# Two heads' scores in turn on half the rows of TensorE, without stacked operands, and all PSUM accumulators from one group of eight banks

## The chip, the core and the metric

One core of a Trainium2 chip runs the whole program, which is one launch. The metric is the device time of that launch in microseconds (us); lower is better. The engines are named as in the profile: PE is TensorE's matmul, PEld its weight load, DVE is VectorE, ACT is ScalarE, POOL is GpSimd, SP is SyncE, which here only issues DMAs. PE writes into PSUM, which has eight banks of 128 x 512 f32.

## The reference

Two layers over 512 tokens of width 1024. Each layer is a half-step SwiGLU, a mixer, and a second half-step SwiGLU, each between two RMS norms. The change lies in the mixer:

```python
proj = u @ w_in[l]
qa, ka, va, qb, kb, vb, qc, kc, vc, gl = jnp.split(proj, split_at, axis=-1)
oa = neighbourhood_attention(qa, ka, va, na_rpb[l])      # 8 heads of 64, windowed, a bias per head
ob = sliding_window_attention(rope(qb), rope(kb), vb, sw_sink[l])   # 8 query heads, 2 kv heads, |i-j| <= 128
oc = differential_attention(rope(qc), rope(kc), vc, lam, ...)       # 4 heads of two maps: p0 - lam * p1, dense
gates = jax.nn.sigmoid(gl + b_gate)
merged = sum(gates[n] * (branch[n] @ w_branch[l, n]) for n in range(3))
h = h + rmsnorm(merged @ w_out[l], mix_post_g[l])
```

All of it is float32. The head width is 64.

## The kernel before

**Precision.** Every operand of a matmul is split into a high and a low part (`split`: ACT writes hi, DVE writes lo = x - hi), and a product is made of hi*hi, hi*lo and lo*hi (`mm3`, lines 298 to 300, PSUM tiles `mm`). A projection of one block of 128 columns is `dense1`: 8 blocks of depth, so 24 matmuls of 128x512. The weights stream in and are split in halves of a tile by ACT (line 199) and DVE (line 200).

**Units of the mixer.** The table `ORDER` lists the units of a mixer, and `do` writes them in that order. `qa`, `qb`, `qc` project q, k, v; `aa`, `ab`, `ac` are the attention units: `aa0` to `aa3` and `ab0` to `ab3` hold a pair of heads each, `ac0` to `ac3` one differential head with two maps. `ga`, `gb`, `gc` are gate projections, `ya`, `yb`, `yc` the branch products, `fc` closes a differential head. A part of the table is `qb0 ga4 ga5 ga7 ya5 ga3 ga6 ab0 qb1 ya1`. In the mixer a scheduler puts the instructions of each engine into a fixed order when the program is built; what is written earlier goes first, as far as its inputs and its buffers are there. Each engine then runs its list in order. In the feed-forward phases and at the mixer's end the order is set by hand.

**PSUM.** `bank(tag)` takes a bank from one of three groups: `mm` (4 banks, projections), `at` (3 banks, scores and transposes) and `o` (1 bank, attention output).

**Scores before.** A head has 64 rows, so `stacks` makes operands of 128 rows by DMA on SP: `st` holds hi over lo, and for k also `sw` with lo over hi. Two matmuls (lines 1337 and 1338, in C 1475 and 1476) then give all four products. `softmax_pv` runs for one head at a time: for each of four blocks of 128 queries the scores, then DVE adds the bias and takes the minimum (line 1341), ACT takes the exponential (1350), DVE scales rows (1357), PE transposes (1365), ACT and DVE split the transposed blocks (324, 325), PE multiplies with v (1368, 1369), and ACT and DVE join the two halves of the output (1371, 1372). B has a sink logit in between (1347, 1353, 1354). `attn_c` takes maxima (1477), scales them (1478), exponentials (1482), joins two maps (1487, 1490), transposes (1498) and multiplies (1501 to 1503). `turn` transposes v on PE (1318) from a copy that `plain` makes on ACT (1425).

Of the kernel before, what the change touches and what calls it, by code (L numbers as in the profile page):

```python
# [2 lines left out]

# [1 line left out]

# [5 lines left out]
F32 = mybir.dt.float32  # L11
F32R = mybir.dt.float32r
# [97 lines left out]
def encoder_kernel(ctx: ExitStack, tc: tile.TileContext, order, xT, wts, cols, rows, rpb, consts, tables, out):  # L110
# [7 lines left out]
    phase = [None]  # L118

    BUFS = {"X": 6, "n": 2, "wr": 3, "wp": 4}  # L120
    ABUFS = {"f": {"t": 4, "x": 10}, "m": {"t": 5, "h": 4, "rr": 2, "tx": 5, "st": 16, "g": 10, "s": 2, "pt": 4}}
    PBUFS = {"mm": 4, "at": 3, "o": 1}

    def open_phase(kind):
        pool = ExitStack()
# [5 lines left out]
    def nm(s):  # L131
        serial[0] += 1
        return f"{s}{serial[0]}"

    def big(tag, dt=F32, shape=(P, T), name="v"):
        if tag in BUFS:
            return sb.tile(list(shape), dt, tag=tag, name=nm(name), bufs=BUFS[tag])
        kind, pool = phase[0]
        return pool.tile(list(shape), dt, tag=tag, name=nm(name), bufs=ABUFS[kind][tag])

# [1 line left out]
        return sb.tile([P, w], F32, tag=tag, name=nm(tag), bufs=bufs)  # L142

    def bank(tag):
        return ps.tile([P, T], F32, tag=tag, name=nm(tag), bufs=PBUFS[tag])

    V, A, G, PE = nc.vector, nc.scalar, nc.gpsimd, nc.tensor

    def f(t):
        return t.bitcast(F32)  # L150
# [1145 lines left out]
        return ap.rearrange("p (j r c) -> p j r c", r=8, j=4)  # L1296


    def stacks(x, both):
        hi, lo = split(x, "tx")  # L1300
        res = []
        for s in range(2):
            own = slice(64 * s, 64 * s + 64)
            st = big("st", F32R, name="st")
            nc.sync.dma_start(f(st)[0:64], f(hi)[own])
            nc.sync.dma_start(f(st)[64:128], f(lo)[own])
            sw = None
            if both:
                sw = big("st", F32R, name="sw")
                nc.sync.dma_start(f(sw)[0:64], f(lo)[own])  # L1310
                nc.sync.dma_start(f(sw)[64:128], f(hi)[own])
            res.append((st, sw))
        return res

    def turn(x, heads):
        tp = bank("at")
# [9 lines left out]
            return lambda j, s: v[j // 2][:, j % 2, s, :]  # L1326
        return split(tp, "st")

    def softmax_pv(sq, sk, vof, bias, scale, sink, odst, oview):
        ss, nmx = [], small("nmx")  # L1330
        sall, at = big("s", shape=(P, NT * T), name="s"), 0
        for i in range(NT):
            j0, j1 = window(i)
            n = (j1 - j0) * P
            sp = bank("at")[:, :n]
            qs = sq[0][:, i * P : (i + 1) * P]
            PE.matmul(sp, qs, sk[0][:, j0 * P : j1 * P], start=True, stop=False)
            PE.matmul(sp, qs, sk[1][:, j0 * P : j1 * P], start=False, stop=True)
            s = sall[:, at : at + n]
            at += n  # L1340
            V.tensor_tensor_reduce(
                out=s, in0=sp, in1=bias(i), scale=-1.0, scalar=3e38, op0=ALU.add, op1=ALU.min,
                accum_out=nmx[:, i : i + 1],
            )
            ss.append(s)
        if sink is not None:
            V.tensor_scalar(out=nmx, in0=nmx, scalar1=scale, scalar2=sink[1], op0=ALU.mult, op1=ALU.min)
        l = small("l")
        for i in range(NT):
            A.activation(ss[i], ss[i], AF.Exp, scale=-scale, bias=nmx[:, i : i + 1], accum_out=l[:, i : i + 1])  # L1350
        if sink is not None:
            es = small("es", 4, 3)
            A.activation(es, nmx, AF.Exp, bias=sink[0])
            V.tensor_tensor(out=l, in0=l, in1=es, op=ALU.add)
        V.reciprocal(out=l, in_=l)
        for i in range(NT):
            V.tensor_scalar(out=ss[i], in0=ss[i], scalar1=l[:, i : i + 1], scalar2=None, op0=ALU.mult)
        op = bank("o")
        for j in range(NT):
            i0, i1 = window(j)  # L1360
            n = (i1 - i0) * P
            tp = bank("at")[:, :n]
            for i in range(i0, i1):
                c = (j - window(i)[0]) * P
                PE.transpose(tp[:, (i - i0) * P : (i - i0 + 1) * P], ss[i][:, c : c + P], ident)  # L1365
# [5 lines left out]
        A.activation(t, op[64:128, :], AF.Copy)  # L1371
        V.tensor_tensor(out=odst, in0=oview(op[0:64, :]), in1=oview(t), op=ALU.add)
# [14 lines left out]
    def mixer(l, op, first):  # L1387
# [40 lines left out]
        OT = {}  # L1428

        def qkv_a(q, k, v):  # L1430
            sq, sk = stacks(plain(q, True, 0.125), False), stacks(plain(k, True), True)
            return sq, sk, turn(plain(v, True), 2)

        oa = [sb.tile([P, 4, T], F32R, tag="X", name=nm("oa"), bufs=BUFS["X"]) for _ in range(2)]

        def attn_a(p, sq, sk, vof):
            o = big("t", name="o")
            for s in range(2):
                softmax_pv(
                    sq[s], sk[s], lambda j, s=s: vof(j, s), biases(2 * p + s), 1.0, None,  # L1440
                    perm(o[64 * s : 64 * s + 64, :]), natural,
                )
# [7 lines left out]
        def attn_b(p, sq, skb, vofb):  # L1450
            o = big("t", name="o")
            for s in range(2):
                hd = 2 * p + s
                kv = hd // 4
                softmax_pv(
                    sq[s], skb[kv], lambda j, kv=kv: vofb(j, kv), bias_b, 0.125,
                    (sink[:, l, hd : hd + 1], nsink[:, l, hd : hd + 1]),
                    o[64 * s : 64 * s + 64, :], lambda ap: ap,
                )
            OT["b", p] = split(o, "g")  # L1460

        oc, totc = [], []

        def attn_c(sq, sk, v):
            vh, vl = v
            aa = []
            sall = big("s", shape=(P, NT * T), name="s")
            for i in range(NT):
                pm = []
                lc = small("lc", 2)  # L1470
                nm2 = small("nm2", 2)
                for s in range(2):
                    sp = bank("at")
                    qs = sq[s][0][:, i * P : (i + 1) * P]
                    PE.matmul(sp, qs, sk[s][0], start=True, stop=False)
                    PE.matmul(sp, qs, sk[s][1], start=False, stop=True)
                    V.tensor_reduce(out=nm2[:, s : s + 1], in_=sp, axis=AX.X, op=ALU.max)
                    V.tensor_scalar(
                        out=nm2[:, s : s + 1], in0=nm2[:, s : s + 1], scalar1=-0.125, scalar2=None, op0=ALU.mult
                    )  # L1480
                    e = big("tx", name="e") if s else sall[:, i * T : (i + 1) * T]
                    A.activation(
                        e, sp, AF.Exp, scale=0.125, bias=nm2[:, s : s + 1], accum_out=lc[:, s : s + 1]
                    )
                    pm.append(e)
                V.reciprocal(out=lc, in_=lc)
                V.tensor_scalar(
                    out=pm[1], in0=pm[1], scalar1=lc[:, 1:2], scalar2=nlam[:, l : l + 1], op0=ALU.mult, op1=ALU.mult
                )
                V.scalar_tensor_tensor(  # L1490
                    out=pm[0], in0=pm[0], scalar=lc[:, 0:1], in1=pm[1], op0=ALU.mult, op1=ALU.add
                )
                aa.append(pm[0])
# [40 lines left out]
                    G.tensor_tensor(out=merged[m], in0=merged[m], in1=t, op=ALU.add)  # L1534

        def qkv_b(c):
            return stacks(rope(dense1(w, l, c, X), cosR, sinR), c == KB)

        def qkv_c(hd):
            sq = stacks(rope(dense1(w, l, QC + hd, X), cosR, sinR), False)  # L1540
            sk = stacks(rope(dense1(w, l, KC + hd, X), cosR, sinR), True)
            return sq, sk, turn(plain(dense1(w, l, VC + hd, X), False), 1)

        def finish_c(hd):
            A.activation(totc[hd], totc[hd], AF.Sqrt)
# [37 lines left out]
        for u in ORDER.split():  # L1583
# [1 line left out]
        M = [split(merged[m], "st", 0.5) for m in range(KD)]  # L1585


        hN = [big("s", shape=(P, 2, 2, T), name="h") for _ in range(2)]
# [4 lines left out]
        H = Handover(  # L1593
            l, "mix_post_g", (1.0, 1.0), ("ffn2_pre_g", l), gains, lambda tb, n: hN[tb // 2][:, tb % 2, n, :],
            lambda tb, n: ys[tb][n], True, [accs[0:2], accs[2:4]] * 2,
        )
        at = len(order) // HB
# [126 lines left out]
```

## Time and profile before

| | |
|---|---|
| median of 3 runs | 2442.7 us (2439.57 to 2444.72) |
| profiled execution, its own time | 2441.57 us |
| its span (first to last instruction) | 2439.8 us |
| PE busy | 2404.1 us (99%) |
| DVE busy | 1797.8 us (74%) |
| ACT busy | 1347.5 us (55%) |
| DMA queue issues of `st` and `sw` from SP | 84 + 84 + 36 + 36 |

PE's busy time is a union of records whose ends are modelled, so the distance from the start of one matmul to the start of the next is what a matmul costs in a stream. For DVE and ACT a record ends after the next has begun, by some 0.08 us on DVE.

### The profile page before, as it was taken

Reading aid. Unit: us, or ns where it says so; the run is one execution under the profiler, and the core shown is the slowest. Engines: PE = TensorE matmul, PEld = TensorE weight load, DVE = VectorE, ACT = ScalarE, POOL = GpSimd, SP = SyncE. Lnnn points to the kernel's source line nnn. Section 1 sums busy time; section 2 is a strip of 40 time slices with the busy share of each in tenths; the row PEclk is TensorE's granted clock in tenths of the full one; section 3 lists DMA queues with packets and bytes.
Section 4 is the critical chain, followed back from the end, with each engine's and each line's share of the span. In section 5 each row is a group of like instructions: output and inputs, shape, how many; then the busy total and the mean of one; then the engine's idle time right before and its main releaser. Section 6 shows DMA issues by size and latency. Waiting matters only on the chain. (4 is left out here: it accounts for less than half of the span.)

```text
span 2439.8 us, 37786 instructions
## 1 busy us (share of the span) xinstructions
PE 2404.1 (99%) x14298; PEld 2111.5 (87%) x14298; DVE 1797.8 (74%) x2943; ACT 1347.5 (55%) x2471; POOL 192.1 (8%) x192
## 2 busy tenths in 40 slices
PE   9999999999999999999999999999999999999998
PEld 8999888888877889998899998888877778899987
DVE  8887976857667467888878878776676764788786
ACT  6555655646555365555655555555465554555553
POOL 0111000000111100110001110000001111011100
PEclk9999999999999999999999999999999999999999
DMA  5566536445442334654435565373454333356642
GB/s 170 162 163 182 169 132 175 116 113 149 111 131 95 111 105 132 169 154 162 170 95 157 156 173 190 116 183 106 113 143 124 110 103 121 96 147 165 184 144 87
DMA packets 119190, 340.59 MB, mean 140 GB/s; under 512 B 15968, under 2 KB 22752, under 8 KB 118496
## 3 DMA queue, kind: packets, MB, share of 16 engines
q1 hardware_dynamic: 91344, 224.85, 29.9%
q10 hardware_dynamic: 22032, 79.78, 10.9%
q0 software_dynamic: 5632, 33.56, 6.8%
q8 instruction: 112, 1.84, 0.3%
q14 instruction: 70, 0.57, 0.1%
HBM read 285.16 MB, written 48.23 MB: 137 GB/s over the span
## 5 line engine op out<-in xcount | busy, mean ns | idle before, releaser
L298 PE MATMUL mm<-X,w 128*128 128x512 f32 (+1 forms) x1044 | 397.1, 380 | 2.2 <-ACT w L199 1.7
L299 PE MATMUL mm<-X,w 128*128 128x512 f32 (+1 forms) x1044 | 396.8, 380 | 0.7 <-DVE X L522 0.7
L300 PE MATMUL mm<-X,w 128*128 128x512 f32 (+1 forms) x1044 | 396.1, 380 | 0.0
L200 DVE TENSOR_TENSOR w<-wr,w 128x512 fp32r<-128x512 f32 x360 | 255.3, 714 | 168.2 <-ACT w L199 167.0
L199 ACT ACTIVATE w<-wr 128x512 fp32r<-128x512 f32 x360 | 223.4, 627 | 226.6 <-PE mm L300 184.3
L842 PE MATMUL mm<-ht,l 128*128 128x256 f32 x1120 | 316.5, 283 | 0.0
L842 PE MATMUL mm<-ht,h 128*128 128x256 f32 x1120 | 316.3, 282 | 0.0
L842 PE MATMUL mm<-lt,h 128*128 128x256 f32 x1120 | 315.6, 282 | 0.0
L298 PEld LDWEIGHTS mm<-X,w 128*128 128x128 f32 x1044 | 197.4, 189 | 34.0 <-ACT w L199 1.9
L299 PEld LDWEIGHTS mm<-X,w 128*128 128x128 f32 x1044 | 197.2, 189 | 32.2 <-DVE X L522 1.1
L300 PEld LDWEIGHTS mm<-X,w 128*128 128x128 f32 x1044 | 197.1, 189 | 31.4
L842 PEld LDWEIGHTS mm<-ht,l 128*128 128x128 f32 x1120 | 213.1, 190 | 0.0
L842 PEld LDWEIGHTS mm<-ht,h 128*128 128x128 f32 x1120 | 213.0, 190 | 0.0
L842 PEld LDWEIGHTS mm<-lt,h 128*128 128x128 f32 x1120 | 212.7, 190 | 0.0
L1082 PE MATMUL mm<-wh,f 128*128 128x512 f32 x640 | 200.3, 391 | 0.0
L842 PE MATMUL mm<-X,h 128*128 128x256 f32 x1120 | 200.3, 279 | 0.0
L842 PEld LDWEIGHTS mm<-X,h 128*128 128x128 f32 x1120 | 171.2, 189 | 0.3
L842 PE MATMUL mm<-X,l 128*128 128x256 f32 x560 | 155.4, 278 | 0.0
L1082 PEld LDWEIGHTS mm<-wh,f 128*128 128x128 f32 x640 | 120.3, 188 | 26.9
L702 DVE TENSOR_TENSOR l<-wr,h 128x1024 fp32r<-128x1024 f32 x70 | 85.7, 1224 | 78.5 <-PE mm L842 78.5
L1082 PE MATMUL mm<-wl,f 128*128 128x512 f32 x320 | 126.6, 396 | 3.1 <-DVE wl L959 3.1
L324 ACT ACTIVATE hi<-at 128x256 fp32r<-128x256 f32 (+2 forms) x168 | 77.2, 474 | 73.4 <-PE at L1365 37.9
(366 smaller groups left out, 5458.5 us busy)
## 6 DMA issues: line engine op xcount, KB each, us to landing
wr<-in_wts_dram SPq DMA_DIRECT2D x223, 512.0 KB, 4.7
wr<-in_wts_dram ACTq DMA_DIRECT2D x152, 512.0 KB, 3.6
sum<-in_wts_dram POOLq DMA_DIRECT2D x64, 512.0 KB, 5.5
st<-hi SPq DMA_DIRECT2D x84, 128.0 KB, 2.5
st<-lo SPq DMA_DIRECT2D x84, 128.0 KB, 3.4
ap<-in_wts_dram SPq DMA_DIRECT2D x20, 512.0 KB, 6.7
a<-kept SPq DMA_DIRECT2D x32, 256.0 KB, 5.9
ap<-sum SPq DMA_DIRECT2D x16, 512.0 KB, 4.7
```

What stands on the lines that cost most here:

```text
L199: A.activation(hi, raw, AF.Copy)
L200: V.tensor_tensor(out=lo, in0=raw, in1=f(hi), op=ALU.subtract)
L298: PE.matmul(acc, w[0], x[0], start=start, stop=False)
L299: PE.matmul(acc, w[0], x[1], start=False, stop=False)
L300: PE.matmul(acc, w[1], x[0], start=False, stop=stop)
L324: A.activation(hi, src, AF.Copy)
L702: V.tensor_tensor(out=W[g]["l1"], in0=raws[g][0], in1=f(W[g]["h1"]), op=ALU.subtract)
L842: PE.matmul(acc, ws[i], xs[j], start=start and k == n == 0, stop=stop and k == HK - 1 and n == 2, skip_group_check=True,)
L1082: PE.matmul(acc, x[i], w[j], start=start and n == 0, stop=stop and n == 2, skip_group_check=True)
```

## The change

`stacks` goes. `parts` splits q and k into hi and lo and leaves them where they are, two heads on 64 rows each; only B's shared k is doubled by DMA (`kv`, two heads' worth of the same 64 rows). `scores` writes six matmuls for a pair of heads, three products each, alternating between rows 0 to 63 and rows 64 to 127, each queued behind the one before with `issue_after`. `attend` writes the scores and minima of both heads for all four query blocks first, and then `softmax_pv` for one head and for the other. `bank` takes every accumulator from one group of eight. Tile `s` is narrower and comes three times, `tx` six times. `ORDER` stays.

```diff
-    PBUFS = {"mm": 4, "at": 3, "o": 1}
+BANKS = 8
+SW = 10 * P
...
     def bank(tag):
-        return ps.tile([P, T], F32, tag=tag, name=nm(tag), bufs=PBUFS[tag])
+        return ps.tile([P, T], F32, tag="bank", name=nm(tag), bufs=BANKS)
...
-    def stacks(x, both):
-        hi, lo = split(x, "tx")
...
+    def parts(x, twice=False):
+        if not twice:
+            return split(x, "st")
...
+    def scores(q, k, i, ks):
+        out = [bank("at")[:, : ks.stop - ks.start] for _ in range(2)]
+        queue = []
+        qs = slice(i * P, (i + 1) * P)
+        for n, (x, y) in enumerate(((0, 0), (0, 1), (1, 0))):
+            for s in range(2):
+                own = slice(64 * s, 64 * s + 64)
+                with tc.issue_after(queue[-1]) if queue else nullcontext():
+                    mm = PE.matmul(out[s], q[x][own, qs], k[y][own, ks], start=n == 0, stop=n == 2)
+                queue.append(mm.ins)
+        return out
...
+    def attend(q, k, vof, bias, scale, sinks, odst, oview):
+        ss, nmx = [[], []], [small("nmx") for _ in range(2)]
+        sall, at = [big("s", shape=(P, SW), name="s") for _ in range(2)], 0
+        for i in range(NT):
+            j0, j1 = window(i)
+            n = (j1 - j0) * P
+            for s, sp in enumerate(scores(q, k, i, slice(j0 * P, j1 * P))):
+                ss[s].append(sall[s][:, at : at + n])
+                V.tensor_tensor_reduce(
+                    out=ss[s][i], in0=sp, in1=bias[s](i), scale=-1.0, scalar=3e38, op0=ALU.add, op1=ALU.min,
+                    accum_out=nmx[s][:, i : i + 1],
+                )
+            at += n
+        for s in range(2):
+            softmax_pv(ss[s], nmx[s], lambda j, s=s: vof(j, s), scale, sinks and sinks[s], odst[s], oview)
```

In the changed file the line numbers are a little higher: the scores are line 1322, the transposes 1377, the products with v 1380 and 1381; in C the transposes are 1502, the products 1505 to 1507.

**PE at `ab0` of layer 0.** `at` are score and transpose banks, `mm` a projection's bank, `s` the softmax rows, `o` the output's bank. Before, the last scores of the first head and what follows, up to the first transposes:

```order
L1338 MATMUL at_5521<-sw_5110,st_5315 128x384
L1337 MATMUL at_5525<-st_5107,st_5315 128x256
L1338 MATMUL at_5525<-sw_5110,st_5315 128x256
L298 MATMUL mm_5663<-X_3642,w_5477 128x512
L299 MATMUL mm_5663<-X_3643,w_5477 128x512
L300 MATMUL mm_5663<-X_3642,w_5477 128x512
...
L299 MATMUL mm_5663<-X_3645,w_5494 128x512
L1365 MATMUL at_5544<-cons,s_5512 128x128
L1365 MATMUL at_5553<-cons,s_5512 128x128
```

Now:

```order
L1322 MATMUL at_5500<-kv_5067,hi_5271 128x256
L1322 MATMUL at_5499<-kv_5068,hi_5271 128x256
L1322 MATMUL at_5500<-kv_5068,hi_5271 128x256
L1322 MATMUL at_5499<-kv_5067,lo_5272 128x256
L1322 MATMUL at_5500<-kv_5067,lo_5272 128x256
L1377 MATMUL at_5524<-cons,s_5467 128x128 x2
L1380 MATMUL o_5523<-hi_5527,v_5119 128x256
L1377 MATMUL at_5533<-cons,s_5467 128x128 x2
L1381 MATMUL o_5523<-lo_5528,v_5119 128x256
```

Before, 23 matmuls of a projection stand between the first head's last score and its first transpose; now the 24 scores of both heads stand in one piece and the first transpose comes right behind them. The next projection's first matmul stands 21 rows further on, among the second head's products with v.

**PE at `ac0` of layer 0.** `s` holds the joined maps of two query blocks, `hi`, `lo` of `o` are split transposes. Before, among the last scores:

```order
L1475 MATMUL at_6887<-st_6669,st_6615 128x512
L1476 MATMUL at_6887<-sw_6672,st_6615 128x512
L300 MATMUL mm_6983<-hi_5938,w_6813 128x512
L1475 MATMUL at_6893<-st_6675,st_6618 128x512
L1476 MATMUL at_6893<-sw_6678,st_6618 128x512
L298 MATMUL mm_6983<-hi_6405,w_6813 128x512
...
L1498 MATMUL at_6904<-cons,s_6830 128x128
L298 MATMUL mm_7001<-X_3642,w_6966 128x512
```

Now:

```order
L1322 MATMUL at_6826<-hi_6609,lo_6562 128x512
L1322 MATMUL at_6827<-hi_6609,lo_6562 128x512
L1502 MATMUL at_6845<-cons,s_6762 128x128 x2
L1502 MATMUL at_6845<-cons,s_6763 128x128 x2
L1505 MATMUL o_6844<-hi_6850,hi_6653 128x512
L1502 MATMUL at_6857<-cons,s_6762 128x128 x2
L1502 MATMUL at_6857<-cons,s_6763 128x128 x2
```

Before, branch products and projections stand between scores and transposes and among the transposes; now nothing does, from the first score of the unit to its sum of squares (line 1515), which is the last of the unit on PE. The other eleven attention units of a mixer read the same way (where two attention units follow each other in `ORDER`, the scores of the second are mixed into the last products of the first), and so does `turn`: its transposes stand right behind the last matmul of the projection that they turn.

**DVE at `ab0`.** `nmx` are the row minima, `l` the row sums, `es` the sink's term. Before, the first head's last minima and what follows:

```order
L1341 ISA s_5512,nmx_5511<-at_5525,cons 128x256
L1341 ISA nmx_5511 128x1
L200 TENSOR_TENSOR w_5681<-wr_5679,w_5681 128x512
L1347 TENSOR_SCALAR nmx_5511<-nmx_5511,nsink 128x4
L1354 TENSOR_TENSOR l_5530<-l_5530,es_5535 128x4
L1355 RECIPROCAL l_5530<-l_5530 128x4
```

Now, with `s_5467` for the first and `s_5468` for the second head:

```order
L1349 ISA s_5467,nmx_5465<-at_5499,cons 128x256
L1349 ISA nmx_5465 128x1
L1349 ISA s_5468,nmx_5466<-at_5500,cons 128x256
L1349 ISA nmx_5466 128x1
L1359 TENSOR_SCALAR nmx_5465<-nmx_5465,nsink 128x4
L1359 TENSOR_SCALAR nmx_5466<-nmx_5466,nsink 128x4
L1366 TENSOR_TENSOR l_5510<-l_5510,es_5515 128x4
L1367 RECIPROCAL l_5510<-l_5510 128x4
```

The second head's minima have moved ahead of the first head's sums and scaling. One split of a weight (line 201) stands among the eight minima of this unit.

The order of PE in the feed-forward phases is the same as before. SP issues 16 DMAs for `kv` in place of 240 for `st` and `sw`.

More of the change, by code (lines that the diff above doesn't have):

```diff
@@ L1 @@
 import math
-from contextlib import ExitStack
+from contextlib import ExitStack, nullcontext
 import numpy as np
@@ L1296, in natural @@
         return ap.rearrange("p (j r c) -> p j r c", r=8, j=4)
-    def stacks(x, both):
-        hi, lo = split(x, "tx")
+    def parts(x, twice=False):
+        if not twice:
+            return split(x, "st")
+        own = split(x, "tx")
         res = []
         for s in range(2):
[L1303 to L1312, printed above, removed]
-        return res
+            pair_ = [big("st", F32R, name="kv") for _ in own]
+            for dst, src in zip(pair_, own):
+                for at in range(2):
+                    nc.sync.dma_start(f(dst)[64 * at : 64 * at + 64], f(src)[64 * s : 64 * s + 64])
+            res.append(tuple(pair_))
+        return res
+    def scores(q, k, i, ks):
[9 more added lines that the diff above has]
+        return out
     def turn(x, heads):
@@ L1334, in softmax_pv @@
             n = (j1 - j0) * P
[L1335 to L1339, printed above, removed]
-            at += n
[L1341 to L1345, printed above, removed]
+            for s, sp in enumerate(scores(q, k, i, slice(j0 * P, j1 * P))):
[4 more added lines that the diff above has]
+                )
+            at += n
+        for s in range(2):
+            softmax_pv(ss[s], nmx[s], lambda j, s=s: vof(j, s), scale, sinks and sinks[s], odst[s], oview)
+    def softmax_pv(ss, nmx, vof, scale, sink, odst, oview):
         if sink is not None:
@@ L1430, in qkv_a, with attn_a @@
         def qkv_a(q, k, v):
-            sq, sk = stacks(plain(q, True, 0.125), False), stacks(plain(k, True), True)
-            return sq, sk, turn(plain(v, True), 2)
+            return parts(plain(q, True, 0.125)), parts(plain(k, True)), turn(plain(v, True), 2)
         oa = [sb.tile([P, 4, T], F32R, tag="X", name=nm("oa"), bufs=BUFS["X"]) for _ in range(2)]
-        def attn_a(p, sq, sk, vof):
+        def attn_a(p, q, k, vof):
             o = big("t", name="o")
[L1438 to L1442, printed above, removed]
+            attend(
+                q, k, vof, [biases(2 * p + s) for s in range(2)], 1.0, None,
+                [perm(o[64 * s : 64 * s + 64, :]) for s in range(2)], natural,
+            )
             OT["a", p] = tuple(t[:, p, :] for t in oa)
@@ L1448, in bias_b, with attn_b, attn_c @@
             return maskB[:, P:] if i == 0 else maskB[:, : 2 * P] if i == NT - 1 else maskB
-        def attn_b(p, sq, skb, vofb):
+        def attn_b(p, q, kb, vofb):
             o = big("t", name="o")
[L1452 to L1459, printed above, removed]
+            kv = p // 2
+            attend(
+                q, kb[kv], lambda j, s: vofb(j, kv), [bias_b] * 2, 0.125,
+                [(sink[:, l, hd : hd + 1], nsink[:, l, hd : hd + 1]) for hd in (2 * p, 2 * p + 1)],
+                [o[64 * s : 64 * s + 64, :] for s in range(2)], lambda ap: ap,
+            )
             OT["b", p] = split(o, "g")
         oc, totc = [], []
-        def attn_c(sq, sk, v):
+        def attn_c(q, k, v):
             vh, vl = v
             aa = []
-            sall = big("s", shape=(P, NT * T), name="s")
+            sall = [big("s", shape=(P, SW), name="s") for _ in range(2)]
             for i in range(NT):
@@ L1471, in attn_c @@
                 nm2 = small("nm2", 2)
[L1472 to L1476, printed above, removed]
+                for s, sp in enumerate(scores(q, k, i, WHOLE)):
                     V.tensor_reduce(out=nm2[:, s : s + 1], in_=sp, axis=AX.X, op=ALU.max)
@@ L1480, in attn_c @@
                     )
[L1481 removed]
+                    e = big("tx", name="e") if s else sall[i // 2][:, i % 2 * T : i % 2 * T + T]
                     A.activation(
@@ L1585, in mixer @@
         M = [split(merged[m], "st", 0.5) for m in range(KD)]
-        hN = [big("s", shape=(P, 2, 2, T), name="h") for _ in range(2)]
+        hN = []
+        for _ in range(NT - 1):
+            h = big("s", shape=(P, SW), name="h")
+            hN.append([h[:, :T], h[:, T : 2 * T]])
+        hN.append([big("tx", name="h") for _ in range(2)])
         ys = [[big(tag, name="y") for tag in ("h", "t")] for _ in range(NT)]
```

14 lines of the change are left out of this document (5 added, 9 removed).

## The prediction

> **What bounds the kernel now.** I read the page first, then the busy time of the two mixers, PE's waits, and then one attention unit instruction by instruction.
>
> ```profile
> span 2439.8 us, 37786 instructions
> PE 2404.1 (99%) x14298; PEld 2111.5 (87%) x14298; DVE 1797.8 (74%) x2943; ACT 1347.5 (55%) x2471; POOL 192.1 (8%) x192
> 360.00:800.00 440.00, 431.79 (x2154) 354.65 (x2154) 297.62 (x686) 243.19 (x531) 33.50 (x23) 1.00 0.46 127
> 1573.00:2015.00 442.00, 433.90 (x2142) 354.95 (x2141) 297.15 (x684) 244.19 (x532) 35.55 (x24) 1.00 0.46 128
> PE at L1337 <- DVE nmx L1341: 2.7, 2, 1.5
> ```
>
> The third and fourth rows are the two mixers: length, then busy time of PE, PEld, DVE, ACT. PE is idle for 440.00 - 431.79 = 8.2 us in one and 8.1 us in the other, 16.3 us in all. So PE sets the time, in the mixers too, and a wait of a score for the softmax before it costs 2.7 us in the whole run. The next rows say what a matmul costs in a stream: the chain of waits merges equal pieces, and 24 of 512 columns take 5.51 us (0.230 each), 72 of 256 take 8.47 us (0.118), 8 transposes 0.90 us (0.11).
>
> ```profile
> 1556.09 5.51 PE mm L1082 x24
> 2146.39 8.47 PE mm L842 x72
> 1688.33 0.90 PE at L1365 x8
> ```
>
> Why PE does not wait is seen at `ab0`, first PE, then DVE and ACT (start, duration, both in us):
>
> ```profile
> 519.99 0.28 PE L1338 MATMUL at<-sw,st 128*128 128x256 f32 x1
> 520.11 0.34 PE L1337 MATMUL at<-st,st 128*128 128x384 f32 x1
> 520.46 0.34 PE L1337 MATMUL at<-st,st 128*128 128x384 f32 x1
> ...
> 521.02 0.28 PE L1338 MATMUL at<-sw,st 128*128 128x256 f32 x1
> 521.14 0.39 PE L298 MATMUL mm<-X,w 128*128 128x512 f32 x1
> ...
> 526.16 0.39 PE L299 MATMUL mm<-X,w 128*128 128x512 f32 x1
> 526.39 0.87 PE L1365 MATMUL at<-cons,s 128*128 128x128 f32 x6
> ```
>
> ```profile
> 520.31 0.42 DVE L1341 CUSTOM_DVE_ANT_0 s<-at,cons 128x256 f32<-128x256 f32 x1 [1.60 <-PE at L1338]
> 520.66 0.56 DVE L1341 CUSTOM_DVE_ANT_0 s<-at,cons 128x384 f32<-128x384 f32 x1
> ...
> 522.57 0.22 DVE L1347 TENSOR_SCALAR nmx<-nmx,nsink 128x4 f32<-128x4 f32 x1
> 525.34 0.16 DVE L1354 TENSOR_TENSOR l<-l,es 128x4 f32<-128x4 f32 x1 [2.55 <-ACT es L1353]
> 522.83 0.51 ACT L1350 ACTIVATE s<-s,nmx 128x256 f32<-128x256 f32 x1 [1.54 <-DVE nmx L1347]
> 525.03 0.28 ACT L1353 ACTIVATE es<-nmx,sink 128x4 f32<-128x4 f32 x1
> ```
>
> From the last score (521.02) to the first transpose (526.39) lie 5.4 us: minima, sink, four exponentials, sums, scaling. PE fills them with the 23 projection matmuls that its order has there. That filling is what the change takes away: in the new order of PE the scores are followed by the transposes at once, in every attention unit, and PE runs its list in order. One group of eight banks, handed out in the order of the code, lets no later projection take a bank ahead of an earlier transpose.
>
> **The change part by part.** I take the three kinds of unit as they would run with nothing between them. From the rows above, 384 columns cost 0.175 a matmul (520.11 to 520.46 for two). The other durations are these; on DVE the next starts 0.08 us before a record ends (520.31 + 0.42 against 520.66), so I take that off.
>
> ```profile
> L1477 DVE TENSOR_REDUCE nm<-at 128x1 f32<-128x512 f32 x64 | 42.7, 682 | 7.3 <-PE at L1476 7.3
> L1490 DVE SCALAR_TENSOR_TENSOR s<-s,lc,e 128x512 f32<-128x512 f32 x32 | 26.4, 825 | 0.1
> L1487 DVE TENSOR_SCALAR e<-e,lc,misc 128x512 f32<-128x512 f32 x32 | 17.9, 559 | 0.1
> L1482 ACT ACTIVATE e<-at,nm 128x512 f32<-128x512 f32 x32 | 21.9, 685 | 10.4 <-DVE nm L1478 10.4
> L325 DVE TENSOR_TENSOR lo<-at,hi 128x512 fp32r<-128x512 f32 x40 | 26.9, 686 | 16.4 <-ACT hi L324 15.7 <-PE at L1498 0.7
> L325 DVE TENSOR_TENSOR lo<-at,hi 128x384 fp32r<-128x384 f32 x64 | 34.6, 550 | 0.7 <-ACT hi L324 0.7
> L1357 DVE TENSOR_SCALAR s<-s,l 128x384 f32<-128x384 f32 x64 | 23.8, 414 | 0.0
> L1357 DVE TENSOR_SCALAR s<-s,l 128x256 f32<-128x256 f32 x64 | 22.4, 350 | 0.9
> L1372 DVE TENSOR_TENSOR o<-o,ot 64x512 f32<-64x512 f32 x32 | 21.8, 681 | 4.3 <-ACT ot L1371 4.0
> L1410 DVE TENSOR_TENSOR bedge<-braw,mask 128x256 f32<-128x256 f32 x32 | 12.5, 417 | 8.7 <-DMA braw<-in_rpb_dram 8.7
> L1425 ACT ACTIVATE x<-mm 128x512 f32<-128x512 f32 x30 | 17.6, 588 | 4.3 <-PE mm L300 4.2
> ```
>
> PE's own work in a pair of heads before: 16 scores 8 x 0.118 + 8 x 0.175 = 2.3, 20 transposes 2.2, 16 products with v 2.3: 6.9 us. After it has 24 scores on half the rows. No row shows a matmul on 64 rows. The bounds are full spacing for each (12 x 0.118 + 12 x 0.175 = 3.5 us) and two at a time (1.75 us). I take full spacing, since every pair of matmuls in the trace follows at it. For C: 24 x 0.230 = 5.5 us, or 2.75, against 16 x 0.230 = 3.7. This matters little here, since the end of the unit hangs on DVE: two at a time starts the first minimum earlier by half of four spacings, 0.24 us in a pair and 0.46 in C, in all 16 x 0.24 + 8 x 0.46 = 7.5 us. The Trainium skill (TensorE: Matmul & The Clock Gate, Part 3 on row tiling) says that matmuls on different row groups run concurrently; by it, this 7.5 us would come off the forecast; no run here shows it yet.
>
> *B (`ab`), time from the first score.* The first minimum starts at 4 x 0.118 + 0.32 = 0.8 (from score 519.99 to minimum 520.31). DVE then runs eight minima, 4 x 0.35 + 4 x 0.48 = 3.3, and the one weight split among them, 0.6: 4.7. The sink is 0.08 later, the first exponential 0.26 after it (522.57 to 522.83), the sums 2.51 after that (522.83 to 525.34), the first transpose 1.05 after those (525.34 to 526.39): 8.6 us, of which PE scores for 3.5 and waits for 5.1. On ACT the second head's exponentials follow the first's sink term, so its sums come 2.51 + 0.3 after the first head's, at 10.4. From there DVE has a reciprocal 0.2, three scalings 0.27 + 0.33 + 0.33, three low parts 0.47 + 0.47 + 0.34, a scaling 0.27, a low part 0.34, an addition 0.6 and three low parts 1.28: 4.9, so the last product starts at 15.4. Five projection matmuls stand among the last products (1.15 us of PE's other work). The unit costs 15.4 - 1.15 - 6.9 = 7.4 us more than before; four of them 29.6.
>
> *A (`aa`), two units in a row.* There is no sink, exponentials follow the minima one by one, and the first transpose waits less: minima start at 0.95 behind the split of v, the first head's fourth ends at 4.2, its exponential with the sum at 4.9, reciprocal and two scalings at 5.9; PE waits 2.4. After that DVE is the longest queue until the second unit's last low part: 16 minima 6.6, 16 scalings 4.8, 16 low parts 6.5, three additions 1.8, a low part of `oa` 0.6, four and five pieces of bias (each 0.34 or 0.47) 3.45, a split of v and reciprocals 0.75: 24.5. With its start (0.95) and the wait for an exponential 25.7, less 1.15 of projections, less 2 x 6.9: 10.8 us more a pair of units, 21.6 a mixer.
>
> *C (`ac`).* The first maximum starts at 4 x 0.230 + 0.39 (the record of a matmul of 512) = 1.3. DVE: 8 maxima 4.8, 8 small scalings and 4 reciprocals 1.0 (some 0.08 each, an estimate from the 0.08 to 0.16 of the small records above), 4 scalings 1.9, 4 joins 3.0 = 10.7, and at its end a wait of 0.9 for the last exponential (0.69 and its sum): 12.9. PE has scored until 5.5 and waits nearly all of the rest. Then transposes 0.4, a high part 0.6, four low parts one after another 2.5, last products 0.9, a square 0.65, four sums of squares 0.45: 18.2 us. PE's work before was 3.7 + 16 x 0.11 + 12 x 0.230 + 0.45 = 8.6: 9.6 more a unit, 38.4 a mixer.
>
> *`turn`.* Its transposes now wait for the copy on ACT: 0.39 (the record of the last matmul) + 0.59 - 0.23 + 0.05 = 0.8; nine a mixer, 7.2 us.
>
> *What goes.* 224 of 240 DMAs on SP. In the list of PE's waits none is ended by `st` or `sw`: projections covered them, and where that cover is gone, the operands now come from ACT and DVE directly. I credit nothing. The narrower `s` and the sixth `tx` cost nothing: the same instructions fill them. ACT and DVE have the same work. The feed-forward phases keep their order.
>
> Sum: 29.6 + 21.6 + 38.4 + 7.2 = 96.8 a mixer, 193.6 for two, less the 16.3 us that PE was idle there before: +177. The profiled execution took 2441.57 us (1.8 more than its span, 1.1 less than the median), so 2619 us.
>
> **The rivals.**
>
> *PE keeps its cover (the other side).* If a projection still filled the waits and two scores ran at a time, scores would fall from 128 x (0.118 + 0.175 + 0.230) = 66.9 to 50.2 us: 2425 us. It decides at a mean wait of 16.7 / 24 = 0.7 us a unit. The 5.4 us at `ab0` and the order of PE speak against it; 3 in 100.
>
> *The clock falls in the waits.* The first matmuls of the run went at half speed, then at full:
>
> ```profile
> 1.00 4.21 PE L292 MATMUL o<-ones 128*128 128x128 f32 x18 [1.00 <-POOL eps L271]
> 6.50 0.42 PE L299 MATMUL mm<-X,w 128*128 128x256 f32 x1
> 6.72 0.42 PE L300 MATMUL mm<-X,w 128*128 128x256 f32 x1
> 7.34 0.28 PE L299 MATMUL mm<-X,w 128*128 128x256 f32 x1
> 7.46 0.28 PE L300 MATMUL mm<-X,w 128*128 128x256 f32 x1
> 10.74 0.39 PE L298 MATMUL mm<-X,w 128*128 128x256 f32 x1 [1.68 <-ACT w L199]
> ```
>
> 256 columns were 0.22 apart until 6.9 us and 0.12 after, so 5.9 us at half speed lost 3 us. If each of the 16 units of B and C brought this back, that is 16 x 3 = 48 us: 2667. Against it, a wait of 1.68 us did not, and no longer one occurs in the trace; the waits here would be 2.4 (A), 5.1 (B) and up to 7.4 broken by single transposes (C); and part of a slow stretch would lie beside DVE. The Trainium skill (TensorE: Matmul & The Clock Gate, Part 1 and the table of goals) has this as its rule: idle for a window of about 3.4 us drops PE to half. The trace agrees for the start; no wait here is long enough to show the rest. 28 in 100, with the near case that ACT and DVE fall behind with weights after a unit (2 us each, the same 48).
>
> *Only the first waits stay*, and behind them PE runs at its own speed: 4 x 5.1 + 4 x 2.4 + 4 x 7.4 + 7.2 = 67, and the added scores 8 x 1.2 + 4 x 1.8 = 17, two times less 16.3: +151, 2593, inside the likeliest. Still less, because DVE is faster alone than beside a full load: below 2560; 12 in 100.
>
> **How the numbers follow.** The likeliest, 2619 with its own range of 2565 to 2650, has 55 in 100; 28 lie above, 12 between 2500 and 2565, 3 are the other side, 2 anything else. The range of 2545 to 2690 leaves out no more than 2 in 10. What a measurement can tell from no change is about 0.2% (5 us). Faster 0.03, the same 0.01, slower 0.96.
>
> **What would show it.** In the new profile PE's busy share falls, by about 177 us of idle in the mixers; the list of PE's waits is led by the transposes behind DVE's `s` (lines 1377 and 1502), and by the products behind `lo`; from the first score of `ab0` to its last product lie about 15 us, in `ac0` about 18. DVE and ACT keep their busy time. In the mixers full-size matmuls that start 0.46 apart would show the clock rival. If the transposes of `ab0` start less than 2 us after its last score, the prediction is wrong at its root.

## The result, and the profile after

The changed kernel takes 2726.1 us (median of 4 runs, 2719.7 to 2726.3) where the kernel before, on the same chip, takes 2442.6. The ratio is 1.1155, 95% interval 1.1135 to 1.1175. The forecast was 2619 with a range of 2545 to 2690: the sign and the main cause were right, the size was 107 us short. The profiled execution took 2719.73 us.

First the page of the changed kernel (span, busy time, and the granted clock in 40 slices), then its two mixers (length, busy PE, PEld, DVE, ACT and POOL, granted clock, DMA's busy share, GB/s):

```profile
span 2718.0 us, 37694 instructions
PE 2497.8 (92%) x14490; PEld 2169.9 (80%) x14490; DVE 1805.2 (66%) x2943; ACT 1360.9 (50%) x2471; POOL 191.3 (7%) x192
PEclk9999998888888899999999999889889889999999
```

```profile
360.00:935.00 575.00, 475.55 (x2224) 381.37 (x2223) 298.45 (x681) 247.34 (x526) 31.86 (x22) 0.88 0.23 70
1715.00:2285.00 570.00, 470.08 (x2198) 376.07 (x2198) 297.51 (x680) 248.02 (x528) 33.38 (x23) 0.89 0.24 71
```

PE is idle for 2718.0 - 2497.8 = 220.2 us, 184.5 more than before. The mixers' clock was 1.00 before and is 0.88 and 0.89 now. In short stretches the clock reads 1.00 or 0.50 (560.2 to 562: 1.00; 732 to 737: 0.50), so time at half speed counts half in that mean. It is 2 x 0.12 x 575 = 138 us in the one and 2 x 0.11 x 570 = 125 in the other, 263 in all. DVE and ACT have the work they had, within 1%. The list of PE's waits (total, times, longest) is led by the rows that were named (the products wait behind ACT's `hi`, 11.2 and 6.4 us, and hardly behind `lo`):

```profile
PE at L1377 <- DVE s L1369: 83.7, 16, 6.8
PE at L1502 <- DVE nm L1482: 29.4, 16, 3.3
PE at L1502 <- DVE s L1494: 27.6, 16, 2.0
PE at L1329 <- ACT x L1437: 19.8, 16, 5.1
```

PE at `ab0`:

```profile
560.23 0.50 PE L1322 MATMUL at<-kv,hi 64*128 64x256 f32 x4
...
561.96 0.29 PE L1322 MATMUL at<-kv,lo 64*128 64x256 f32 x2
568.38 0.80 PE L1377 MATMUL at<-cons,s 128*128 128x128 f32 x2 [6.12 <-DVE s L1369]
...
570.67 1.05 PE L1377 MATMUL at<-cons,s 128*128 128x128 f32 x4
...
578.15 0.39 PE L1381 MATMUL o<-lo,v 128*128 128x256 f32 x1
```

Where 23 projection matmuls stood, PE now waits 6.12 us. The first transpose comes 8.15 us after the first score; the last product at 17.9 us. From the first score to the start of the last pair it is 1.7 us: the scores run two at a time. The four transposes at 570.67 last 1.05 us where eight took 0.90 before: half speed.

The end of `ac0`, first on ACT, then on PE:

```profile
731.70 0.60 ACT L325 ACTIVATE hi<-at 128x512 fp32r<-128x512 f32 x1 [2.13 <-PE at L1502]
734.03 0.60 ACT L325 ACTIVATE hi<-at 128x512 fp32r<-128x512 f32 x1 [1.74 <-PE at L1502]
736.16 0.60 ACT L325 ACTIVATE hi<-at 128x512 fp32r<-128x512 f32 x1 [1.54 <-PE at L1502]
738.30 0.60 ACT L325 ACTIVATE hi<-at 128x512 fp32r<-128x512 f32 x1 [1.54 <-PE at L1502]
```

```profile
718.45 0.50 PE L1322 MATMUL at<-hi,hi 64*128 64x512 f32 x2
...
731.18 0.48 PE L1502 MATMUL at<-cons,s 128*128 128x128 f32 x1 [1.97 <-DVE s L1494]
732.35 0.79 PE L1505 MATMUL o<-hi,hi 128*128 128x512 f32 x1 [0.69 <-ACT hi L325]
732.94 1.27 PE L1502 MATMUL at<-cons,s 128*128 128x128 f32 x5
...
741.82 1.87 PE L1515 MATMUL at<-ones,sqt 128*128 128x1 f32 x8 [1.41 <-ACT sqt L1512]
743.54 0.77 PE L299 MATMUL mm<-hi,w 128*128 128x512 f32 x1
```

The high parts come 2.1 to 2.3 us apart, though each takes 0.60. The transposes of the second block (732.94) stand behind the product of the first (732.35), which waits for ACT: transposes, high part, product, next transposes, in series. The unit leaves PE at 743.54, 25.1 us after its first score.

### The profile page after: what moved, and what is told of

It is laid out like the page before. It is cut to its first block, busy times and chain, and to the rows that moved or that the text cites. A ratio compares the mean times of both kernels' runs of the same rounds, so it can differ in the third digit from the quotient of the medians.

```text
span 2718.0 us, 37694 instructions
## 1 busy us (share of the span) xinstructions
PE 2497.8 (92%) x14490; PEld 2169.9 (80%) x14490; DVE 1805.2 (66%) x2943; ACT 1360.9 (50%) x2471; POOL 191.3 (7%) x192
## 5 line engine op out<-in xcount | busy, mean ns | idle before, releaser
L300 PEld LDWEIGHTS mm<-X,w 128*128 128x128 f32 x1044 | 197.5, 189 | 35.6 <-DVE X L523 1.1
L1377 PE MATMUL at<-cons,s 128*128 128x128 f32 x320 | 79.4, 380 | 83.7 <-DVE s L1369 83.7
L326 DVE TENSOR_TENSOR lo<-at,hi 128x256 fp32r<-128x256 f32 (+2 forms) x168 | 89.1, 536 | 75.2 <-ACT hi L325 56.4
```

The costliest lines, as they stand in the source:

```text
L300: PE.matmul(acc, w[0], x[1], start=False, stop=False)
L326: V.tensor_tensor(out=lo, in0=src, in1=f(hi), op=ALU.subtract)
```

## The experiments

The theory after this result: one group of banks, handed out in the order of the code, takes the cover away (all of the loss); on top of the waits lie a half-speed PE and an order of PE that is serial at the units' ends. Its rivals: the scores of two heads in one piece take the cover away, or ACT and DVE are too slow for them.

**Half speed taken out.** Matmuls that nobody reads, behind the scores:

```diff
+        keep_warm(bank("at"), 25 if sinks else 15)
         for s in range(2):
             softmax_pv(...)
...
+                    if j == 0:
+                        keep_warm(idle, (9, 6, 5, 8)[i])
                     PE.transpose(tp[:, i * P : (i + 1) * P], aa[i][:, j * P : (j + 1) * P], ident)
```

> The changed kernel with matmuls added that nobody reads: operands X, 512 columns, into a free bank, right behind the scores of each attention unit (15 in an A unit, 25 in a B unit, 28 in a C unit ahead of its four first transposes), so that PE works through waits that it idles through now. The order of all else stays. Theory (waits of 185 us, and on top of them a half-speed TensorE after each): the waits stay, the granted clock of the mixers goes back to 0.98 or more, and the time falls by what the slow stretches cost, some 95 to 110 us: 2600 to 2640. Rival 1 (half speed costs little, because it lies beside DVE and ACT, and the missing 100 us are waits of another kind): 2700 to 2740. Rival 2 (the added matmuls themselves delay the transposes): above 2740.

2691.9 us, ratio 1.1029 (1.1008 to 1.1049): 34 us less, not 95 to 110. The clock is nearly back, first the two mixers' windows as above, and at `ab0` nothing is late for the added matmuls:

```profile
360.00:935.00 575.00, 533.50 (x2557) 420.98 (x2556) 302.53 (x689) 251.64 (x535) 35.74 (x24) 0.97 0.25 73
1715.00:2285.00 570.00, 527.92 (x2503) 414.21 (x2502) 301.55 (x688) 250.22 (x532) 38.78 (x26) 0.98 0.25 72
```

```profile
562.04 5.97 PE L1319 MATMUL at<-X 128*128 128x512 f32 x25
568.22 0.66 PE L1386 MATMUL at<-cons,s 128*128 128x128 f32 x2 [0.21 <-DVE s L1378]
...
576.73 0.39 PE L1390 MATMUL o<-lo,v 128*128 128x256 f32 x1
```

The unit is 16.7 us long instead of 17.9. By clocks of 0.97 and 0.98, 2 x 0.03 x 575 + 2 x 0.02 x 570 = 57 us at half speed are left, so some 206 of the 263 us went, and 34 us of time with them. (The added matmuls cost a little in their turn: the first pair of A units lasts 35.6 us, 33.9 without them.) The slow stretches are not mostly waits: over the whole trace of the changed kernel PE's records cover 181 of the 273 us at clock 0.50. But a unit's end is a series of work on PE, ACT and DVE, and a faster PE shortens only its own links of it; that is an argument, and no run takes it apart. Each theory had a part: the slow stretches are real, but PE's busy time in them is not what they cost.

**The banks alone.** The kernel before, with its stacks, and one group of eight banks:

```diff
-        return ps.tile([P, T], F32, tag=tag, name=nm(tag), bufs=PBUFS[tag])
+        return ps.tile([P, T], F32, tag="bank", name=nm(tag), bufs=BANKS)
```

> The kernel before, with its stacks and one head at a time, and only the accumulators changed: one group of eight banks in place of groups of 4, 3 and 1. Theory (the group of banks takes the projections' cover away, whatever the form of the scores): a head now waits for its own softmax before its first transpose, and there are 16 such waits a mixer in A and B where the changed kernel has 8, so as slow as the changed kernel or slower: 2700 to 2950, with the granted clock under 0.93 in the mixers. Rival (the two heads' scores in one piece take the cover away, the banks are not to blame): 2440 to 2500, clock 1.00.

2922.5 us, ratio 1.1965 (1.1947 to 1.1983): slower than the change as a whole. Its waits are in the places of the changed kernel: the transposes wait for `s` 32 times instead of 16, and those of `turn` (line 1318) 98.4 us instead of 19.8:

```profile
PE at L1365 <- DVE s L1357: 159.0, 32, 13.4
PE at L1318 <- ACT x L1425: 98.4, 16, 12.0
```

**The scores alone.** The changed kernel, and groups of 4, 3 and 1 again (the same two lines the other way):

> The changed kernel with its scores on 64 rows in turn, and the accumulators again from three groups of 4, 3 and 1 banks. Theory (the group of banks costs all, the scores on 64 rows gain): projections stand between scores and transposes again, the clock stays at 1.00, and the scores take less: 2 x 16 us less at most if all of them run two at a time, so 2415 to 2445. Rival 1 (the scores' form costs too: pairs are torn apart, two heads' softmax in one piece uses up the three banks, PE waits): 2450 to 2550. Rival 2 (the scores of two heads in one piece are what takes the cover away): 2600 to 2730.

2476.8 us, ratio 1.0140 (1.0125 to 1.0155), clock 1.00 in both mixers. The banks therefore cost the changed kernel 249 us. But the scores, far from gaining 16.7 us, lose 35, which is the first rival's case, not the theory's. PE's row of the page, then PE in layer 0:

```profile
PE 2442.6 (99%) x14490; PEld 2104.1 (85%) x14490; DVE 1800.7 (73%) x2943; ACT 1348.5 (55%) x2471; POOL 188.9 (8%) x192
```

```profile
394.08 0.40 PE L301 MATMUL mm<-X,w 128*128 128x512 f32 x1
394.41 0.43 PE L1324 MATMUL at<-hi,hi 64*128 64x384 f32 x1
394.78 0.50 PE L302 MATMUL mm<-X,w 128*128 128x512 f32 x1
395.21 0.44 PE L1324 MATMUL at<-hi,hi 64*128 64x384 f32 x1
```

PE is busy 2442.6 - 2404.1 = 38.5 us longer than before. Around the lone score, 394.08 to 394.41 is 0.33 where a projection's matmul takes 0.23, the score takes 0.37 (0.175 in the rows of before), and the next projection matmul 0.43. The scheduler has set the 576 scores in 128 pieces among projections, and each piece loses at both ends.

**The price of a change of rows, by itself.** Matmuls of zeros added to the kernel before, in the middle of projections, 252 in all; on 64 rows, and on 128:

```diff
+                if name in ("w_in", "w_branch") and i is None and k in (1, 4):
+                    PE.matmul(acc[:, :P], nought[:64], w[0][:64], start=False, stop=False)
```

> The kernel before, with one matmul of 128 columns on 64 rows added behind two of the eight depth blocks of each projection and one of four in each branch product of the mixers (252 in all): its weights are zeros and it adds into the projection's own bank, so that the result stays. Theory (each change between matmuls on 128 and on 64 rows holds the queue up, 0.09 to 0.20 us going in and 0.2 to 0.28 coming out, as the pieces of scores among projections showed): about 0.4 us each, 100 us: 2525 to 2560. Rival (the loss in those pieces comes from something else, torn pairs or late operands): 0.06 to 0.11 each, 2455 to 2475.

> The same with the added matmuls on all 128 rows. Both theories: 0.11 us each, 252 of them 28 us: 2465 to 2476. If it is much slower than that, the price of the 64 rows is that of an added matmul of another kind, not of the change of rows.

2544.8 us on 64 rows, ratio 1.0418 (1.0400 to 1.0436), and 2483.2 on 128, ratio 1.0171 (1.0148 to 1.0193). That is 101 / 252 = 0.40 us for a visit to 64 rows, as expected, and 39 / 252 = 0.16 for the same matmul on all rows, more than the 0.11 (28 us) that was expected. First on 64 rows, then on 128:

```profile
397.13 0.39 PE L300 MATMUL mm<-X,w 128*128 128x512 f32 x1
397.45 0.32 PE L317 MATMUL mm<-w,nought 64*128 64x128 f32 x1
397.70 0.50 PE L298 MATMUL mm<-X,w 128*128 128x512 f32 x1
398.04 0.39 PE L299 MATMUL mm<-X,w 128*128 128x512 f32 x1
```

```profile
401.33 0.39 PE L300 MATMUL mm<-X,w 128*128 128x512 f32 x1
401.56 0.22 PE L317 MATMUL mm<-w,nought 128*128 128x128 f32 x1
401.61 0.45 PE L298 MATMUL mm<-X,w 128*128 128x512 f32 x1
401.90 0.39 PE L299 MATMUL mm<-X,w 128*128 128x512 f32 x1
```

The loss is 0.09 us going in (0.32 against 0.23), some 0.2 coming out (0.25 against 0.05), and 0.11 in the first full matmul (0.34 against 0.23), of which half stands on 128 rows too (0.29 from 401.61 to 401.90). Without the added matmul's own 0.055 (an estimate: half of a transpose's 0.11), a visit to 64 rows costs 0.35 us; the difference between the two kernels' times is less, 0.40 - 0.16 = 0.24. With 0.35 the kernel of three groups can be added up: 128 pieces x 0.35 = 45; 92 of the pieces hold an odd number of scores, one of them without a partner, for which half a mean spacing is lost (the scores, 192 each of 512, 384 and 256 columns, take 192 x (0.230 + 0.175 + 0.118) / 2 = 50 us two at a time, 0.09 each), 8; less 16.7: +36. Measured: +34.6. With 0.24 it would be +22; so the sum speaks for 0.35, but its terms were not measured one by one.

**The two heads' scores not in turn.** Three groups of banks, and the three products of one head ahead of the other's:

```diff
-        for n, (x, y) in enumerate(((0, 0), (0, 1), (1, 0))):
-            for s in range(2):
+        for s in range(2):
+            for n, (x, y) in enumerate(((0, 0), (0, 1), (1, 0))):
```

> The kernel with three groups of banks and scores on 64 rows, with one thing changed: the three products of the one head are written ahead of the three of the other, not in turn. Theory (two matmuls run side by side only if neighbours in the queue stand on different halves of the rows): scores take their full spacing, 50 us more work; it was 2477, so 2500 to 2530. Rival (the two halves overlap in any order, or not at all): 2465 to 2490.

2478.1 us, ratio 1.0147 (1.0131 to 1.0162): no difference, against the theory. PE's program has the 384-column scores of one head here, all three, then the six of 256:

```profile
395.57 0.44 PE L1324 MATMUL at<-hi,hi 64*128 64x384 f32 x2
395.81 0.38 PE L1324 MATMUL at<-lo,hi 64*128 64x256 f32 x2
395.93 0.43 PE L1324 MATMUL at<-hi,lo 64*128 64x256 f32 x2
```

Each row of `x2` joins one score of 384 and one of 256 columns (the row shows one of the two shapes): the next score on the other rows starts 0.01 us after the first of 384, ahead of the second and third of 384. So the halves overlap without alternation. The comparison is not pure: the order gave 102 pieces in place of 128, which would save 26 x 0.35 = 9 us, while 36 pieces of three scores have no partners, which would cost about as much (36 x 3 x 0.09 = 10).

**The units' ends.** The changed kernel, with all transposes of a head ahead of its first product (C alike):

```diff
+        tps = []
         for j in range(NT):
...
-            tp = bank("at")[:, :n]
+            tps.append(bank("at")[:, :n])
...
+        for j in range(NT):
-            hi, lo = split(tp, "pt", shape=(P, n))
+            hi, lo = split(tps[j], "pt", shape=(P, n))
```

> The changed kernel with one thing moved: the transposes of all four blocks of a head (in C, of a unit) are written ahead of the first product with v, so that on TensorE no group of transposes stands behind a product that waits for ScalarE and VectorE. Theory (a unit's end is longer than VectorE's queue, because each block's transposes wait behind the product of the block before: 1.3 to 1.6 us a block in C where the low part alone takes 0.6): C ends 2 to 3 us sooner, A and B 1 to 2 us, over 8 and 16 units 32 to 56 us less: 2670 to 2695. Rival (the ends are VectorE's work, in whatever order TensorE stands): 2715 to 2735.

2680.7 us, ratio 1.0977 (1.0961 to 1.0994): 45 us less, as the theory had it. In `ac0` on ACT and on PE:

```profile
722.97 1.08 ACT L325 ACTIVATE hi<-at 128x512 fp32r<-128x512 f32 x2 [2.13 <-PE at L1507]
725.18 0.60 ACT L325 ACTIVATE hi<-at 128x512 fp32r<-128x512 f32 x1 [1.12 <-PE o L1512]
726.46 0.60 ACT L325 ACTIVATE hi<-at 128x512 fp32r<-128x512 f32 x1 [0.68 <-PE o L1512]
```

```profile
722.46 1.11 PE L1507 MATMUL at<-cons,s 128*128 128x128 f32 x4 [1.33 <-DVE s L1498]
730.90 0.48 PE L299 MATMUL mm<-hi,w 128*128 128x512 f32 x1
```

The four high parts start within 3.5 us, not 6.6, and PE goes on 8.4 us after the last wait for `s`, where it was 743.54 - 731.18 = 12.4.

**Both together.** The same, and the added matmuls:

> Two of the parts together, to close the account: the changed kernel with matmuls that nobody reads behind the scores (alone 34 us off) and with the transposes of all blocks ahead of the products (alone 45 us off). Theory (the half-speed stretches and the order at the units' ends are two separate terms, added to what was forecast): 2726 - 34 - 45 = 2647, within 2635 to 2660, and what remains to the forecast of 2619 is a third, smaller term. Rival (both shorten the same wait): 2665 to 2685.

2660.7 us, ratio 1.0898 (1.0879 to 1.0916): 65 us less than the changed kernel, a microsecond outside the theory's bounds; the two overlap by 14 us.

**The cover given back.** Eight banks in one group and pieces of 24 scores stay; only the order of writing changes. Behind the scores the first three matmuls of a projection are written, then the tail of the attention unit, then the rest of the projection:

```diff
                 mm3(acc if i is None else acc[:, HALVES[i]], w, x, k == 0, k == len(X) - 1)
+            if inner:
+                inner.pop()()
...
-qb0 ga4 ga5 ga7 ya5 ga3 ga6 ab0 qb1 ya1
+ga7 qb0 ab0 tb0:ga3,ga6 tb0:qb1 ya5 ab1 tb1:ya1,ya2 tb1:ya6
```

(`tb0:ga3,ga6` begins `ga3`, then `ga6`, then writes the first head's tail, then ends them.)

> The changed kernel, with eight banks in one group and scores on 64 rows in one piece of 24, and the order of writing changed: behind a unit's scores the first three matmuls of one or two projections are written, then the transposes and products of a head (in C, of the unit), then the rest of those projections, so that a projection has its bank before the transposes have theirs. Theory (the order in which one group hands out its banks takes the cover away, and nothing else does): projections fill the waits, the clock is back at 0.99 to 1.00, idle time of TensorE falls from 220 us to 60 to 110, the time to 2450 to 2540. Rival (VectorE and ScalarE cannot give softmax and weights fast enough when the scores of two heads come in one piece): above 2600.

> Both of these together: projections begun behind the scores, and the transposes of all four blocks ahead of the products. Theory: as the one before, with the ends of the units shorter by 1 to 2 us each: 2425 to 2500, since pieces of 24 scores on 64 rows lose only some 0.35 us a piece at their two ends and run two at a time between (24 x 0.35 = 8 us against 16.7 us saved). Rival (the ends are VectorE's work): within 10 us of the kernel with the projections alone.

2576.7 us, ratio 1.0548 (1.0532 to 1.0564), and 2545.5 with the transposes ahead, ratio 1.0420 (1.0403 to 1.0438). The order of writing alone gives back 149 us, but both miss their ranges. In the second the waits for `s` are nearly gone, and others lead:

```profile
PE at L1326 <- ACT hi L329: 40.9, 6, 10.0
PE at L1333 <- ACT x L1446: 20.0, 16, 5.2
```

Scores wait for a q that the same order had projected too late, and `turn` for its copy. The last version moves these too:

> The kernel with projections begun behind the scores and all transposes ahead of the products, which ran in 2545 us, with the two waits gone that its trace still shows: scores behind the high part of q (42 us; the units that project q for B stand one or two units sooner), and the transposes of v behind ScalarE's copy (20 us; v is projected first, and its transposes are written behind the first three matmuls of the next projection), and a third projection under three of the C units. Theory (the waits were all a matter of the order in which banks are handed out, and scores on 64 rows in pieces of 24 are themselves cheaper by 16.7 - 24 x 0.35 = 8 us): granted clock 1.00, TensorE idle under 70 us, 2430 to 2475. Rival (with the cover back, ScalarE and VectorE fall behind with weights and q): 2485 to 2540.

2508.5 us, ratio 1.0266 (1.0250 to 1.0284): 218 us of the 283 are given back, yet by the rival's range, not the theory's. PE is idle 2507.0 - 2421.9 = 85.1 us; the waits are many and small (the three largest sums are 15.8, 14.0 and 11.4 us, in 6, 12 and 6 waits):

```profile
PE 2421.9 (97%) x14490; PEld 2112.1 (84%) x14490; DVE 1796.6 (72%) x2943; ACT 1347.4 (54%) x2471; POOL 190.8 (8%) x192
```

No run divides the 65 us by which this version is still slower than the kernel before. No version made from the changed kernel beats the kernel before.

## Why the prediction was right or wrong

*The root, no cover.* Right. The transposes of `ab0` start 6.4 us after its last score, and idle time rose by 184.5 us against +177. The agreement is partly luck: at half speed some of what are waits counts as busy. With the clock held (but for some 57 us), the kernel is still 250 us slower than before, so the waits and ends together were too small by up to 73.

*Up to the first transpose.* Right: 5.65 us in `aa0` for 5.9, 8.15 in `ab0` for 8.6; the last `s` of `ac0` at 12.7 (731.18 - 718.45) for 12.9.

*From there to the unit's end.* This is the step that failed. I took DVE's queue as the bound ("four low parts one after another 2.5", "4.9, so the last product starts at 15.4"). In PE's order, which the section on the change shows (two transposes, a product, two transposes), each block's transposes stand behind a product that waits for ACT. `ab0` took 9.8 us from there, not 6.8 (8.5 at full speed); `ac0` 12.4, not 5.3. In C I also left out the copy of `o` on DVE (0.69 us), which comes ahead of the square, and my terms from there add up to 5.5, not 5.3. A has the same fault: its first pair, from the first score to the start of the last product (length, busy PE, PEld, DVE, ACT and POOL, clock, DMA),

```profile
390.65:424.53 33.88, 22.99 (x127) 18.20 (x126) 26.84 (x85) 19.95 (x55) 0.00 (x0) 0.80 0.15 47
```

lasts 33.9 us where I took 25.7, and DVE, the bound that I took, is idle for 7 of them; 1.6 of these it waits for a piece of the bias by DMA. Moving the transposes gives back 45 us.

*Full clock.* The second error: the likeliest case had none of the slow stretches. The rival had them, priced at 48 us; with the clock held 34 come off. Its arguments against were wrong in two points. "No longer one occurs in the trace" is a misreading. At the end of the kernel before, PE waits 2.85 us, and four transposes then take 1.01 us, where four took 0.60 shortly before; the clock from 2434 on is 0.50:

```profile
2423.51 0.60 PE L512 MATMUL at<-cons,a 128*128 128x128 f32 x4
2433.77 1.01 PE L512 MATMUL at<-cons,a 128*128 128x128 f32 x4 [2.85 <-DVE a L464]
```

And in `ac0` no wait is over 2.2 us, single transposes stand between, and PE is slow behind them nevertheless (five transposes in 1.27 us at 732.94; the full-size matmuls behind the unit start 0.43 apart, the sign that the prediction named for this rival). The Trainium skill (TensorE: Matmul & The Clock Gate, Part 1) has the clock at half after an idle window of about 3.4 us; the wait of 6.12 us at `ab0` agrees. Here waits of 2.15, 1.43, 1.24 and 1.97 us with single transposes between them (`ac0`) were enough.

*What remains.* The two errors together give back 65 us, and 2619 + 65 = 2684 leaves 42 to the 2726. The traces say where they lie. Measured as in the prediction, the units of the changed kernel are 103 us longer than forecast: the pairs of A 32 (33.9, 32.5, 35.8 and 32.4 for 25.7), B 25, C 46 (23.2 to 25.1 each for 18.2). `turn` has 5 more: 19.8 us of waits for 9 x 0.8 x 2 = 14.4, since the copy for B's v stands 5 us behind others on ACT. That makes 108, as much as the forecast was short. In the run with both changes the units are still 45 us over: A 20 (17 of them in the first pair of each mixer), B 9 and C 16, so there is no third term outside them. What in them makes these 45 no run shows.

*Scores at full spacing.* Wrong, and of little effect. Pairs run side by side (the 24 scores of `ab0` start within 1.7 us, not 3.5), and the first transposes (in C, the last `s`) come some 0.2 to 0.45 us sooner than forecast. Of the time that this saves PE little is left, by an estimate: the changed kernel has 42 pieces of scores, at 0.35 us some 15, nearly the 16.7 us that they save.

*The other side (2425).* Its mechanism fails twice: the cover is gone, and with the cover there it would not have been faster, as the kernel of three groups shows.

*"DVE is faster alone than beside a full load."* Hardly: the split of a weight (128x512) takes 714 ns on average before and 700 now, the maxima of C 682 in both.

*Nothing for the 224 DMAs.* No run here separates them.

## What to carry to other kernels

Where a scheduler hands out buffers of one group in the order of the code, as here, a later projection does not pass an earlier transpose, however free PE is: separate groups, or a projection begun ahead of the waiting work, keep the cover. A unit without cover is not as long as its busiest queue; follow the order of the waiting engine, block by block, for products that stand ahead of the next block's first step. Matmuls on half the rows paid only in long pieces: here a piece must save more than 0.24 to 0.35 us, and six scores of 512 columns (an estimate: 0.69 instead of four full matmuls, 0.92) save 0.23.

## What the runs showed of the hardware

Going from 128 to 64 rows and back cost 0.40 us a visit against 0.16 for the same matmul on 128 rows. Two row halves worked as two queues: in the kernel with scores not in turn, a score of 256 columns on one half (395.59) started ahead of the second score of 384 (395.85), which stood before it in the program, on the other. The Trainium skill (TensorE: Matmul & The Clock Gate, Part 3) says that matmuls start and end in program order; these starts do not agree. After a wait of 2.85 us at the end of the kernel before the clock was at half, after one of 1.68 us near its start it was not. And taking away some 206 us at half clock saved only 34.
